# Order of the expert loop in a mixture-of-experts block: gathers three experts ahead, transposes before the down products

## The chip, the cores and the metric

The kernel runs on one core of a Trainium2 chip (trn2). The metric is the device time of one execution in microseconds (us). Three runs of the kernel before gave a median of 1673.04 us (1669.24 to 1675.33).

## The reference, cut to what matters

The reference is one decoder block: a mixer half (not touched by the change) and a routed mixture of experts over 512 tokens of width 1024. Every token is routed to 8 of 64 experts, and every expert is a SwiGLU layer of hidden width 256:

```python
def expert_block(args):
    toks, ws, e = args
    xb = u_pad[toks]                                             # gather the tokens of this expert
    hid = jax.nn.silu(xb @ we_gate[e]) * (xb @ we_up[e])         # (128, 256)
    return (hid @ we_down[e]) * ws[:, None]                      # (128, 1024), scaled by the routing weight
routed = jax.ops.segment_sum(y_slots, slot_tok, num_segments=N + 1)[:N]
```

All arithmetic is float32. The number of tokens of an expert is known only on the chip.

## The kernel before, in words

The expert loop (`experts`, lines 1075 to 1295) is unrolled over the 64 experts, in an order written out by hand. Each engine runs its own instructions in that order and waits on semaphores for the others. What an expert does depends on its token count `n`, which each engine reads into a register; `tc.If` then gives branches on each engine that has work in them:

- **light** (`n <= 64`): the float32 weights are used as they were loaded. gate and up products in float32 (`gate_up_light`, L976), one copy of the sums to `hid` by ScalarE (L1185), two transposes of `hid` by TensorE (`hidden_in`, L1008), silu and product after them (`hidden_turned`, L1225 and L1226), down products (`down_light`, L985).
- **heavy** (`n > 64`): each of the three weight units (`gu[e][0]`, `gu[e][1]`, `dn[e]`, 1 MB each) is first split into a high and a low float32r part: a copy by ScalarE (L45) and a subtraction by VectorE (L46), 128x2048 each. The products are then three float32r matmuls each (`mm3`, L61 to L63). silu and product stand ahead of the transposes (`gate_act`, L998 and L999), and the transposed hidden values are split again (`hidden_out`, L1014 and L1015).
- **two blocks** (`n > 128`): a heavy expert with a second block of tokens: it is gathered, transposed, multiplied and scattered besides the first.

The tokens of expert `e` are gathered by an indirect DMA on the POOL queue (`fetch`, and `fetch_over` for the second block) into `xg`, transposed by TensorE (`turn_in`, L899, 8 transposes) into the two PSUM buffers of `xt`, and evicted (`turned`: L1202 for a light expert, the split pair L909 and L910 for a heavy one). `downs(e - 1)` is one expert behind: the down products of the first block of the expert before. The result is added into DRAM by an indirect DMA on the POOL queue (`scatter`, L1044). The loads of expert `e + 2` are issued by SyncE at the end of the iteration (L946, L947, L953) into 8 raw buffers of 1 MB, used in turn, three for each expert.

In iteration `e` the order before is: gathers of `e + 2`; split of the next expert's first unit; products of `e`; second products; transposes of `e + 1`; their eviction and the split of the next expert's second unit, in one branch; transposes of the second block of `e + 1`; down products of `e - 1`; transposes of `hid` of `e`; second down products with their own transposes; scatters; loads. A fifth product (`index_part`, L858, bf16, small) makes the slot numbers of expert `e + 4`.

Where a value is written in only one of two branches, the other branch counts the semaphore up instead, at its line of `If` (L1160 is that of `by_count`, L1169 of `if_two`, L1176 of `if_heavy`).

Of the kernel before, what the change touches and what calls it, by code (L numbers as in the profile page):

```python
# [11 lines left out]
F32 = mybir.dt.float32  # L12
# [9 lines left out]
P = 128  # L22
T = 512
NT = 4
# [34 lines left out]
def mm3(k, out, sh, sl, mh, ml, first, last):  # L59
    nc = k.nc  # L60
    nc.tensor.matmul(out, sh, mh, start=first, stop=False)  # L61
    nc.tensor.matmul(out, sh, ml, start=False, stop=False)  # L62
    nc.tensor.matmul(out, sl, mh, start=False, stop=last)  # L63
# [788 lines left out]
    return oh  # L852


def slot_product(k, ps, oh, vv, b):

    for t in range(NT):
        k.nc.tensor.matmul(ps[:, b, 0:5], oh[:, t, b, :], vv[:, t, :], start=t == 0, stop=t == NT - 1)  # L858


# [23 lines left out]
def gather(k, idx, b, xg, n=P):  # L884
    k.nc.gpsimd.indirect_dma_start(out=xg[:n], out_offset=None, in_=k.u2d, bounds_check=T - 1, oob_is_err=False,  # L885
                                   in_offset=bass.IndirectOffsetOnAxis(ap=idx[0][:n, b:b + 1], axis=0))
    return xg


def turn_tiles(k):  # L890
    return [k.xt.tile([P, 512], F32, name="xt", tag="xt").rearrange("p (q t) -> p q t", q=4) for _ in range(2)]


def turn_in(k, src, halves):

    xv = src.rearrange("p (q k) -> p k q", k=NK)
    for hf, pv in enumerate(halves):
        for q in range(4):
            k.nc.tensor.transpose(pv[:, q, :], xv[:, hf * 4 + q, :], k.ident)  # L899


def turn_out(k, halves, x, full=None):

    nc = k.nc
    for hf, pv in enumerate(halves):
        ks = slice(hf * 4, hf * 4 + 4)
        if full is not None:
            nc.scalar.copy(full[:, ks, :], pv)
        nc.scalar.copy(x[0][:, ks, :], pv)  # L909
        nc.vector.tensor_sub(x[1][:, ks, :], pv, x[0][:, ks, :].bitcast(F32))  # L910
    return x


def turn(k, src, x, full=None):
    halves = turn_tiles(k)
    turn_in(k, src, halves)
    return turn_out(k, halves, x, full)
# [39 lines left out]
def gate_up_mm(k, x, units, ps=None, halves=(0, 1)):  # L957
    xh, xl = x
    if ps is None:
        ps = k.gu.tile([P, 512], F32, name="gu", tag="gu")  # L960
    for hf in halves:
        h, l = (w.rearrange("p (s k f) -> p k s f", k=4, s=2) for w in (units[hf].h, units[hf].l))
        pv = ps.rearrange("p (s f) -> p s f", s=2)
        for q in range(4):
            kk = hf * 4 + q
            mm3(k, pv, xh[:, kk, :], xl[:, kk, :], h[:, q], l[:, q], kk == 0, kk == NK - 1)
    return ps
# [35 lines left out]
def hidden_in(k, hid, ps=None):  # L1003

    hv = hid.rearrange("p (q j) -> p j q", j=2)
    ps = k.ht.tile([P, 2, P], F32, name="ht", tag="ht") if ps is None else ps
    for j in range(2):
        k.nc.tensor.transpose(ps[:, j, :], hv[:, j, :], k.ident)  # L1008
    return ps


def hidden_out(k, ps, hx):
    nc = k.nc
    nc.scalar.copy(hx[0], ps)  # L1014
    nc.vector.tensor_sub(hx[1], ps, hx[0].bitcast(F32))  # L1015
# [59 lines left out]
def experts(k, shared):  # L1075
    nc, tc, a = k.nc, k.tc, k.a
    ET = mybir.EngineType
    idx, xg, gu, dn, oh, counts = {}, {}, {}, {}, {}, {}
# [42 lines left out]
    def first(e, move):  # L1121
        sized(count(e), (16, 32, 48, 64, 80, 96, 112, P), move)
# [9 lines left out]
    def fetch(e):  # L1132
        if e < E:
            xg[e] = k.xg[e % 2]
            first(e, lambda n: gather(k, idx[e], 0, xg[e], n))

    def fetch_over(e):
        if e < E:
            second(e, lambda n: gather(k, idx[e], 1, k.xg[3 + e % 2], n))
# [13 lines left out]
    every, both = (ET.PE, ET.Activation, ET.DVE), (ET.Activation, ET.DVE)  # L1153

    def by_count(e, engines, light, heavy):

        if e == 0:
            heavy()
        elif e < E:
            with tc.If(count(e, engines) <= LIGHT) as small:  # L1160
                light()
            with small.Else():
                heavy()

    def if_two(e, two, one=lambda: None):

        if e == E:
            return one()
        with tc.If(count(e, every) > P) as more:  # L1169
            two()  # L1170
        with more.Else():
            one()

    def if_heavy(e, engines, body):
        if e < E:
            with tc.If(count(e, engines) > LIGHT):  # L1176
                body()

    def products(e):

        g, hid = k.gu.tile([P, 512], F32, name="gu", tag="gu"), hidden(k)

        def light():
            gate_up_light(k, k.xf, gu[e], g)
            nc.scalar.copy(hid, g[:, :256])  # L1185

        def heavy():
            gate_up_mm(k, k.xT[e % 2], gu[e], g)
            if e > 0:
                dn[e].split(k, k.dnw[e % 2])  # L1190
            gate_act(k, g, hid)

        by_count(e, every, light, heavy)
        return hid

    def turned(e, halves):

        if e == E:
            return
        def light():  # L1200
            for hf, pv in enumerate(halves):
                nc.scalar.copy(k.xf[:, hf * 4:hf * 4 + 4, :], pv[:, :, :LIGHT])  # L1202

        def heavy():
            turn_out(k, halves, k.xT[e % 2])
            gu[e][1].split(k, k.gu1w)

        by_count(e, both, light, heavy)

    def downs(e):  # L1210
        if e < 0:
# [6 lines left out]

        by_count(e, every, lambda: down_light(k, k.hT, dn[e], y, w), heavy)

    def hidden_turned(e, hid):
        ps = hidden_in(k, hid)

        def light():
            nc.scalar.activation(k.hT, ps[:, :, :LIGHT], AF.Silu)  # L1225
            nc.vector.tensor_mul(k.hT, k.hT, ps[:, :, LIGHT:])  # L1226

        by_count(e, both, light, lambda: hidden_out(k, ps, k.hx[e % 2]))

    with tc.manual_schedule():  # L1230
        fetch_over(0)
        fetch_over(1)
        if_two(0, lambda: turn(k, k.xg[3], k.xT[1]))
        for e in range(E):
            fetch(e + 2)
            fetch_over(e + 2)
            onehot(e + 4)
            for i in (e, e + 1):
                if i < E:
                    for engines in (every, both):  # L1240
                        count(i, engines)
            if_heavy(e + 1, both, lambda: gu[e + 1][0].split(k, k.gu0w[(e + 1) % 2]))
            hid = products(e)
            hid1, halves = hidden(k), turn_tiles(k)
            slots = slot_tile(k, 2) if e + 4 < E else None

            def turns():
                if e + 1 < E:
                    turn_in(k, xg[e + 1], halves)

            def second_products():
                gate_act(k, gate_up_mm(k, k.xT[(e + 1) % 2], gu[e]), hid1)
                turns()

            def index_part(b):
                if e + 4 < E:
                    slot_product(k, slots, oh[e + 4], k.V[:, :, e + 4, :], b)

            def next_second():
                index_part(0)  # L1260
                turn(k, k.xg[3 + (e + 1) % 2], k.xT[e % 2])

            def second_down():
                ps = turn_tiles(k)[0].rearrange("p q t -> p (q t)")[:, :2 * P].rearrange("p (j t) -> p j t", j=2)
                hidden_in(k, hid1, ps)
                index_part(1)
                hidden_out(k, ps, k.hx[2])
                for n in range(2):
                    down(k, k.hx[2], dn[e], n, k.xg[2], idx[e][1][:, 1:2])

            if_two(e, second_products, turns)
            turned(e + 1, halves)
            if_two(e + 1, next_second, lambda: index_part(0))
            downs(e - 1)
            hidden_turned(e, hid)
            if_two(e, second_down, lambda: index_part(1))
            if e > 0:
                first(e - 1, lambda n: scatter(k, idx[e - 1], 0, k.yl[(e - 1) % 2], (e - 1) % 2, n))
            second(e, lambda n: scatter(k, idx[e], 1, k.xg[2], e % 2, n))
            load(e + 2)  # L1280
            if e + 4 < E:
                idx[e + 4] = slot_numbers(k, slots, 2)
        e = E - 1
        downs(e)
        first(e, lambda n: scatter(k, idx[e], 0, k.yl[e % 2], 1, n))
        part = k.part = [token_pair(k, k.Y[0], t) for t in (0, 2)]
        for t in range(NT):
            eng = (nc.vector, nc.gpsimd)[t % 2]
            y, h = (u[t // 2][:, t % 2, :] for u in (part, k.hs2))
            eng.tensor_mul(y, y, k.rows[:, 0, :])  # L1290
            eng.tensor_add(h, h, y)  # L1291
# [183 lines left out]
```

## Time and profile before

| | |
|---|---|
| median of three runs | 1673.04 us (1669.24 to 1675.33) |
| the profiled execution, its time | 1673.0 us |
| its span, first to last instruction | 1671.3 us |
| mean granted TensorE clock | 0.947 of full |
| DMA over the span | 340.32 MB, 204 GB/s |
| DMA from 800 to 1630 us (the expert loop) | 230.93 MB, 278 GB/s |

The mixer, the norm, the router and the shared expert end at about 808 us; the expert loop runs from there to about 1628 us, and the output follows. Engines: PE is TensorE's matmul, PEld its weight load, DVE VectorE, ACT ScalarE, POOL GpSimd, SP SyncE. A name with q (DVEq) is the engine's sequencer: a branch or a semaphore.

### The profile page before, as it was taken

Reading aid. Unit: us, or ns where it says so; the run is one execution under the profiler, and the core shown is the slowest. Engines: PE = TensorE matmul, PEld = TensorE weight load, DVE = VectorE, ACT = ScalarE, POOL = GpSimd, SP = SyncE. Lnnn points to the kernel's source line nnn. Section 1 sums busy time; section 2 is a strip of 40 time slices with the busy share of each in tenths; the row PEclk is TensorE's granted clock in tenths of the full one; section 3 lists DMA queues with packets and bytes.
Section 4 is the critical chain, followed back from the end, with each engine's and each line's share of the span. In section 5 each row is a group of like instructions: output and inputs, shape, how many; then the busy total and the mean of one; then the engine's idle time right before and its main releaser. Section 6 shows DMA issues by size and latency. Waiting matters only on the chain. (4 is left out here: it accounts for less than half of the span.)

```text
span 1671.3 us, 25992 instructions
## 1 busy us (share of the span) xinstructions
PE 1475.4 (88%) x8084; PEld 1156.2 (69%) x8084; DVE 1011.8 (61%) x1744; ACT 745.2 (45%) x1027; POOL 370.3 (22%) x312
## 2 busy tenths in 40 slices
PE   5999999999999999999898888898798888887970
PEld 5888788788888778888675666566576665665640
DVE  6889778778877974558743354545436453355326
ACT  3465546454434223325544455444536454355332
POOL 5201101002010111220122322322324222221226
PEclk7999999999999999999999999899899989898995
DMA  9442433243333236236738778958889999898974
GB/s 288 122 126 76 138 102 121 76 126 101 107 105 117 82 114 233 87 115 227 294 113 285 252 235 289 329 189 258 282 251 313 324 329 318 287 325 273 297 288 151
DMA packets 152127, 340.32 MB, mean 204 GB/s; under 512 B 15816, under 2 KB 94832, under 8 KB 142272
## 3 DMA queue, kind: packets, MB, share of 16 engines
q1 hardware_dynamic: 135888, 294.94, 51.8%
q0 software_dynamic: 15408, 40.23, 9.4%
q8 instruction: 118, 1.93, 0.5%
q10 hardware_dynamic: 576, 2.10, 0.3%
q14 instruction: 137, 1.12, 0.2%
HBM read 314.00 MB, written 31.01 MB: 206 GB/s over the span
## 5 line engine op out<-in xcount | busy, mean ns | idle before, releaser
L46 DVE TENSOR_TENSOR wl<-raw,wh 128x2048 fp32r<-128x2048 f32 x114 | 273.5, 2404 | 100.0 <-ACT wh L45 88.4
L45 ACT CAST wh<-raw 128x2048 fp32r<-128x2048 f32 x114 | 216.6, 1906 | 140.3 <-PE mm L62 65.7
L1044 POOL DMA_INDIRECT Y<-yl,idx x64 | 108.2, 1691 | 481.8 <-ACT yl L988 271.9
L61 PE MATMUL mm<-uh,wh 128*128 128x512 f32 x432 | 171.7, 397 | 1.9 <-ACT zs L285 1.9
L63 PE MATMUL mm<-uh,wl 128*128 128x512 f32 x432 | 170.4, 395 | 0.0
L62 PE MATMUL mm<-ul,wh 128*128 128x512 f32 x432 | 169.8, 393 | 0.0
L899 PE MATMUL xt<-ident,xg 128*128 128x128 f32 x632 | 97.2, 300 | 58.2 <-issue 18.6
L899 PEld LDWEIGHTS xt<-ident,xg 128*128 128x128 f32 x632 | 84.9, 196 | 77.7 <-issue 48.9
L976 PE MATMUL gu<-raw,xf 128*64 128x256 f32 x1056 | 125.9, 387 | 6.1 <-DMA raw<-in_we_up_dram 3.5
L885 POOL DMA_INDIRECT xg<-u2d,idx x75 | 93.5, 1247 | 117.5 <-DVE oh L851 36.4
L46 DVE TENSOR_TENSOR pair<-raw,pair 128x2048 fp32r<-128x2048 f32 x33 | 75.0, 2290 | 58.2 <-ACT pair L45 49.7
L976 PEld LDWEIGHTS gu<-raw,xf 128*64 128x64 f32 x1056 | 77.2, 138 | 42.6 <-issue 7.2
L61 PE MATMUL gu<-wh,xh 128*128 128x512 f32 x256 | 103.1, 403 | 1.0 <-ACT xh L909 0.6
L62 PE MATMUL gu<-wl,xh 128*128 128x512 f32 x256 | 101.9, 398 | 0.7 <-DVEq L1169 0.7
L63 PE MATMUL gu<-wh,xl 128*128 128x512 f32 x256 | 101.3, 396 | 0.0
L1226 DVE TENSOR_TENSOR hT<-hT,ht 128x128 f32<-128x128 f32 x33 | 9.5, 288 | 146.8 <-ACTq L1169 142.5
L61 PEld LDWEIGHTS mm<-uh,wh 128*128 128x128 f32 x432 | 81.6, 189 | 20.4 <-ACT zs L285 2.3
L63 PEld LDWEIGHTS mm<-uh,wl 128*128 128x128 f32 x432 | 81.6, 189 | 17.7 <-issue 0.9
L62 PEld LDWEIGHTS mm<-ul,wh 128*128 128x128 f32 x432 | 81.5, 189 | 16.8 <-issue 0.4
L45 ACT CAST pair<-raw 128x2048 fp32r<-128x2048 f32 x33 | 62.1, 1903 | 61.7 <-DMA raw<-in_we_gate_dram 22.8
L985 PE MATMUL yo<-raw,hT 128*64 128x512 f32 x264 | 75.5, 695 | 3.5 <-DMA raw<-in_we_gate_dram 2.0
L327 DVE SCALAR_TENSOR_TENSOR cv<-mm,cw,cv 128x511 f32<-128x511 f32 (+2 forms) x90 | 66.6, 741 | 2.1 <-ACT cv L324 1.8
(354 smaller groups left out, 3336.8 us busy)
## 6 DMA issues: line engine op xcount, KB each, us to landing
raw<-in_we_gate_dram SPq DMA_DIRECT2D x124, 512.0 KB
raw<-in_we_up_dram SPq DMA_DIRECT2D x124, 512.0 KB
raw<-in_we_down_dram SPq DMA_DIRECT2D x62, 1024.0 KB
raw<-in_w_in_dram SPq DMA_DIRECT2D x27, 1024.0 KB
raw<-in_w_ada_dram SPq DMA_DIRECT2D x16, 1024.0 KB
big<-in_w_ada_dram SPq DMA_DIRECT2D x16, 512.0 KB
raw<-in_w_in_dram SPq DMA_DIRECT2D x16, 512.0 KB
raw<-in_w_br_ssd_dram SPq DMA_DIRECT2D x8, 1024.0 KB
```

Of the source, the lines that this page charges most:

```text
L45: nc.scalar.copy(h, raw)
L46: nc.vector.tensor_sub(l, raw, h.bitcast(F32))
L61: nc.tensor.matmul(out, sh, mh, start=first, stop=False)
L62: nc.tensor.matmul(out, sh, ml, start=False, stop=False)
L63: nc.tensor.matmul(out, sl, mh, start=False, stop=last)
L327: nc.vector.scalar_tensor_tensor(cv[:, sft:], ps[:, :T - sft], k.cw[:, j * 32 + blk:j * 32 + blk + 1], cv[:, sft:], op0=ALU.mult, op1=ALU.add)
L885: k.nc.gpsimd.indirect_dma_start(out=xg[:n], out_offset=None, in_=k.u2d, bounds_check=T - 1, oob_is_err=False, in_offset=bass.IndirectOffs ...
L899: k.nc.tensor.transpose(pv[:, q, :], xv[:, hf * 4 + q, :], k.ident)
L976: nc.tensor.matmul(ps[s * LIGHT:(s + 1) * LIGHT, :256], x[:, kk, :], w[:, s, kk % 4, :], start=kk == 0, stop=kk == NK - 1)
L985: nc.tensor.matmul(ps[n * LIGHT:(n + 1) * LIGHT, :], x[:, j, :], unit.raw[:, j * D + n * 512:j * D + n * 512 + 512], start=j == 0, stop=j ...
L1044: k.nc.gpsimd.indirect_dma_start(out=k.Y[acc], out_offset=bass.IndirectOffsetOnAxis(ap=idx[0][:n, b:b + 1], axis=0), in_=y[:n], in_offset= ...
L1226: nc.vector.tensor_mul(k.hT, k.hT, ps[:, :, LIGHT:])
```

## The change

Five things change in the loop; the arithmetic is the same.

1. `fetch` and `fetch_over` are called for `e + 3` near the end of iteration `e` (ahead of its scatters) and no longer for `e + 2` at its start; those of expert 2 are called ahead of the loop.
2. The split of the next expert's first unit moves into the branches of `products`: in a heavy expert it is first, in a light one it comes after the copy of `hid`.
3. The split of the next expert's second unit leaves the branch of `turned` and gets an `If` of its own, behind the second block's hidden transposes.
4. The transposes of `hid` come right after those of the next expert's tokens, ahead of `downs(e - 1)`. Those of a second block come next, into a buffer of `gu` and no longer of `xt`, with their eviction.
5. The transposes of the next expert's second block come after `downs(e - 1)`; the second block's down products are last. The index products are dealt out differently.

```diff
         def light():
             gate_up_light(k, k.xf, gu[e], g)
             nc.scalar.copy(hid, g[:, :256])
+            next_split()
 
         def heavy():
+            next_split()
             gate_up_mm(k, k.xT[e % 2], gu[e], g)
...
-        def heavy():
-            turn_out(k, halves, k.xT[e % 2])
-            gu[e][1].split(k, k.gu1w)
-
-        by_count(e, both, light, heavy)
+        by_count(e, both, light, lambda: turn_out(k, halves, k.xT[e % 2]))
...
+        fetch(2)
+        fetch_over(2)
         for e in range(E):
-            fetch(e + 2)
-            fetch_over(e + 2)
             onehot(e + 4)
...
-            if_heavy(e + 1, both, lambda: gu[e + 1][0].split(k, k.gu0w[(e + 1) % 2]))
             hid = products(e)
...
+            def second_turned():
+                ps = k.gu.tile([P, 512], F32, name="gu", tag="gu")[:, :2 * P].rearrange("p (j t) -> p j t", j=2)
+                hidden_in(k, hid1, ps)
+                index_part(0, (0, 1))
+                hidden_out(k, ps, k.hx[2])
+
             def next_second():
-                index_part(0)
                 turn(k, k.xg[3 + (e + 1) % 2], k.xT[e % 2])
+                index_part(0, (2, 3))
 
             def second_down():
-                ps = turn_tiles(k)[0].rearrange("p q t -> p (q t)")[:, :2 * P].rearrange("p (j t) -> p j t", j=2)
-                hidden_in(k, hid1, ps)
                 index_part(1)
-                hidden_out(k, ps, k.hx[2])
                 for n in range(2):
                     down(k, k.hx[2], dn[e], n, k.xg[2], idx[e][1][:, 1:2])
 
             if_two(e, second_products, turns)
             turned(e + 1, halves)
-            if_two(e + 1, next_second, lambda: index_part(0))
+            ps = hidden_in(k, hid)
+            if_two(e, second_turned, lambda: index_part(0, (0, 1)))
+            if_heavy(e + 1, both, lambda: gu[e + 1][1].split(k, k.gu1w))
             downs(e - 1)
-            hidden_turned(e, hid)
+            hidden_turned(e, ps)
+            if_two(e + 1, next_second, lambda: index_part(0, (2, 3)))
             if_two(e, second_down, lambda: index_part(1))
+            fetch(e + 3)
+            fetch_over(e + 3)
             if e > 0:
```

`next_split()` is `if_heavy(e + 1, both, ...)` with the split of `gu[e + 1][0]`, and `slot_product` takes the token tiles that it is to work on.

## Rows read from the trace of the kernel before

**Rows 1.** Two stretches of the loop; last columns granted clock, DMA share, GB/s.

```profile
800.00:1250.00 450.00, 391.02 (x2199) 291.01 (x2198) 208.96 (x406) 210.55 (x291) 117.41 (x81) 0.94 0.77 255
1250.00:1350.00 100.00, 86.54 (x545) 62.91 (x543) 48.08 (x98) 49.99 (x70) 30.65 (x19) 0.97 0.97 320
```

**Rows 2.** TensorE's waits, 800 to 1630: total us, times, longest.

```profile
PE xt L899 <- issue: 18.6, 6, 5.4
PE xt L899 <- ACT wh L45: 16.1, 6, 6.0
PE ht L1008 <- DVEq L1160: 15.3, 5, 6.2
PE xt L899 <- DMA xg<-u2d,idx: 14.7, 12, 2.4
PE yo L61 <- ACT hh L1014: 10.0, 11, 1.4
PE ht L1008 <- DVEq L1169: 7.7, 4, 3.4
PE xt L899 <- DVE xl L910: 5.7, 1, 5.7
PE xt L1008 <- DVEq L1169: 5.3, 2, 2.7
```

**Rows 3.** Light experts' copy of `hid`: count, shortest/median/longest ns.

```profile
L1185 ACT COPY hid<-gu x33: 366/372/374, 882.5 to 1608.4; 128x256 f32<-128x256 f32 x33
```

**Rows 4.** Load issues' waits on SyncE, 800 to 1630.

```profile
SPq L946 <- PE yo L61: 243.5, 27, 26.7
SPq L946 <- PE yo L985: 144.8, 23, 14.0
```

**Rows 5.** Timeline, two blocks to two blocks (e = 2).

```profile
848.46 0.68 PE L899 MATMUL xt<-ident,xg 128*128 128x128 f32 x4 [1.08 <-ACT xh L909]
...
849.87 0.71 PE L899 MATMUL xt<-ident,xg 128*128 128x128 f32 x4 [0.72 <-ACT wh L45]
```

**Rows 6.** Timeline, light to heavy (e = 50), weights late.

```profile
1467.81 0.37 ACT L1185 COPY hid<-gu 128x256 f32<-128x256 f32 x1
1467.94 2.29 DVE L46 TENSOR_TENSOR pair<-raw,pair 128x2048 fp32r<-128x2048 f32 x1 [11.75 <-ACT pair L45]
...
1470.43 0.67 PE L1008 MATMUL ht<-ident,hid 128*128 128x128 f32 x2 [6.15 <-DVEq L1160]
```

**Rows 7.** Timeline, light to two blocks (e = 10).

```profile
965.33 2.29 DVE L46 TENSOR_TENSOR pair<-raw,pair 128x2048 fp32r<-128x2048 f32 x1 [0.45 <-ACT pair L45]
...
966.27 0.37 ACT L1185 COPY hid<-gu 128x256 f32<-128x256 f32 x1 [0.98 <-PE gu L976]
...
969.35 1.71 PE L899 MATMUL xt<-ident,xg 128*128 128x128 f32 x8 [2.12 <-issue]
...
970.99 3.25 PE L985 MATMUL yo<-raw,hT 128*64 128x512 f32 x8
...
974.61 0.48 PE L61 MATMUL gu<-pair,xh 128*128 128x512 f32 x1
```

**Rows 8.** Timeline, light to heavy (e = 14), weights early.

```profile
1016.03 1.90 ACT L45 CAST pair<-raw 128x2048 fp32r<-128x2048 f32 x1 [0.34 <-ACTq L1169]
...
1018.91 0.37 ACT L1185 COPY hid<-gu 128x256 f32<-128x256 f32 x1 [0.98 <-PE gu L976]
...
1019.80 1.94 PE L985 MATMUL yo<-raw,hT 128*64 128x512 f32 x8
...
1024.14 0.50 PE L63 MATMUL gu<-pair,xl 128*128 128x512 f32 x1 [1.31 <-issue]
```

**Rows 9.** Timeline, heavy to heavy (e = 33).

```profile
1288.50 0.41 DVE L999 TENSOR_TENSOR hid<-hid,gu 128x256 f32<-128x256 f32 x1
1289.06 0.47 PE L1008 MATMUL ht<-ident,hid 128*128 128x128 f32 x2 [2.33 <-DVEq L1169]
```

**Rows 10.** VectorE's waits at passed branches.

```profile
DVE fx L869 <- DVEq L1169: 7.3, 34, 0.5
```

More of the change, by code (lines that the diff above doesn't have):

```diff
@@ L852, in slot_onehot, with slot_product @@
     return oh
-def slot_product(k, ps, oh, vv, b):
-    for t in range(NT):
+def slot_product(k, ps, oh, vv, b, tiles=range(NT)):
+    for t in tiles:
         k.nc.tensor.matmul(ps[:, b, 0:5], oh[:, t, b, :], vv[:, t, :], start=t == 0, stop=t == NT - 1)
@@ L1181, in products, with next_split @@
         g, hid = k.gu.tile([P, 512], F32, name="gu", tag="gu"), hidden(k)
+        def next_split():
+            if_heavy(e + 1, both, lambda: gu[e + 1][0].split(k, k.gu0w[(e + 1) % 2]))
         def light():
@@ L1219, in downs, with hidden_turned @@
         by_count(e, every, lambda: down_light(k, k.hT, dn[e], y, w), heavy)
-    def hidden_turned(e, hid):
-        ps = hidden_in(k, hid)
+    def hidden_turned(e, ps):
         def light():
@@ L1253, in second_products, with index_part @@
                 turns()
-            def index_part(b):
+            def index_part(b, tiles=range(NT)):
                 if e + 4 < E:
-                    slot_product(k, slots, oh[e + 4], k.V[:, :, e + 4, :], b)
+                    slot_product(k, slots, oh[e + 4], k.V[:, :, e + 4, :], b, tiles)
+            def second_turned():
[3 more added lines that the diff above has]
+                hidden_out(k, ps, k.hx[2])
             def next_second():
-                index_part(0)
                 turn(k, k.xg[3 + (e + 1) % 2], k.xT[e % 2])
+                index_part(0, (2, 3))
             def second_down():
-                ps = turn_tiles(k)[0].rearrange("p q t -> p (q t)")[:, :2 * P].rearrange("p (j t) -> p j t", j=2)
-                hidden_in(k, hid1, ps)
                 index_part(1)
-                hidden_out(k, ps, k.hx[2])
                 for n in range(2):
```

## The prediction

> **What bounds the kernel now.** I read the windows first. From 800 to 1250 us TensorE is busy 391 of 450 us and the DMA engines 0.77 of the time; from 1250 to 1350 the DMA share is 0.97 [rows 1]. So neither fills the loop: TensorE is idle for about one eighth of it, and the DMA is the limit only in runs of light experts, where every expert's 3.1 MB take 9.8 us at the 320 GB/s of that stretch. [...]
>
> Then TensorE's waits [rows 2]. The rows of `xt L899` other than the gathers' make some 41 us: 18.6 + 16.1 + 5.7 and a small rest, less one that is another wait. On the timeline nearly all of it stands in front of the second block's transposes, 11 times. `yo <- hh` with 10.0 and `xt L1008` with 5.3 stand in the second block's down part. `ht L1008`, 15.3 + 7.7, is the hidden transposes waiting for VectorE, and 14.7 are gathers that landed late.
>
> Then the order of the experts, walked through on the timeline: 33 are light [rows 3], 20 heavy with one block, 11 have two. A light expert is followed by one of two blocks 6 times, by a heavy one 9 times; three heavy ones are followed by two blocks.
>
> Last, what the loads wait for: 243.5 + 144.8 us of SyncE's time ends with a down product [rows 4]. The three units of expert e + 2 are released in the main by `downs(e - 1)`.
>
> **A wait after an `If`.** One row decides how I cost the reordering. After light expert 50 ScalarE copied `hid` by 1468.18, and VectorE has nothing to do with it; yet TensorE's transposes began at 1470.43, just after VectorE's split of the next expert's unit ended at 1470.23 and it passed its branch (`DVEq L1160`) [rows 6]. So whoever reads a value behind an `If` waits until both engines have counted as far as the longer branch would have. In the new kernel the next split stands inside that branch, behind the copy. I expect the transposes of `hid` to wait for it still, and they now stand ahead of the down products.
>
> **Part A, experts of two blocks (11).** Their hidden transposes come early and their eviction runs under the first block's down products: the 10.0 and the 5.3 go [rows 2]. Where two such follow each other (twice), the second turn no longer waits for the split behind the eviction, 1.08 + 0.72 [rows 5], 3.6 in all. [...] What hides the new order's work: some 2 to 3 us of down products. **-20.**
>
> **Part B, light or heavy to two blocks (9).** The remaining 37 us of waiting at the second turn don't vanish. Take e = 10. Before, the split ran under the products and VectorE ended it at 967.62; the turn then had to wait until 969.35 for the eviction, and the next products began at 974.61 [rows 7]. Now the split starts after the copy: 966.64, a branch 0.35, ScalarE 1.90 [rows 8], 0.1, VectorE 2.29, which makes 971.3. [...] That is 0.7 to 2.5 later; I take 1.5, for the three with early weights. In the six where the split was late anyway, it doesn't start later, and the gap between its end and the second turn (967.62 to 969.35, 1.7) is filled with hidden transposes and down products: 1 to 4 earlier, I take 2. Together 3 x 1.5 - 6 x 2. **-7.5.**
>
> **Part C, light to heavy (9).** Here is the loss. At e = 14 the copy ended at 1019.28; split 0.35 + 1.90 + 0.1 + 2.29 to 1023.9, hidden transposes 0.5, down products 1.94, index 0.24: products from 1026.7, their third matmul 0.7 later at 1027.4. Before it was at 1024.14, a wait of 1.31 included [rows 8]. So 3.3 to 4.5 with the slow clock, 3.5 for each of four with early weights. In the five with late weights the wait was there [rows 6] and only the down products (1.94 to 3) come on top, less what the next products lose today to the clock: 1.5 each. Of the nine, three (two early, one late, 8.5 us) lead into an expert whose own product is late by 6 us or so for want of weights, which takes the loss up. 14 + 7.5 - 8.5. **+13.**
>
> **Part D, heavy experts.** `hid` of e = 33 was done at 1288.91, and the transposes waited only the last 2.33 for it, since the down products came first [rows 9]. With the transposes first that cover is gone. On the timeline about twelve such products come more than a turn (1.05) late. Were each to cost a whole set of down products, it would be 30; but VectorE's sequence is the bound of such runs and stays as it is, so that a run pays once: five runs at about 1. Bounds 0 and 30; nearer to the low one, since the waits of a run don't add up in the trace. **+5.**
>
> **Part E, the gathers.** Issued three ahead, each is on its queue behind the next expert's turn and no longer behind a scatter that waits for the down products. That takes 14.7 off [rows 2], but eight of the twelve stand where part B or C waits anyhow. **-3.5.** Queued behind the gather of a second block are now the scatters, which wait for TensorE's turn; the yl buffers they free are needed two experts later, so nothing.
>
> **Part F, branches.** There is one more `If` for each expert on TensorE and two on ScalarE and VectorE. A passed one holds VectorE 7.3 / 34 = 0.21 [rows 10]. They lie on the path only where part B and C count 0.35 for one; the rest and a tail whose last eviction is queued later: **+2.** [...]
>
> **The sum.** -20 - 7.5 + 13 + 5 - 3.5 + 2 = -11. The profiled execution took 1673.0 (span 1671.3 and 1.7 around it), as much as the median. **1662 us.**
>
> **Rivals.**
>
> *The wait ends with the copy.* If TensorE waits for the copy alone, part C falls to about 0 and part B grows to what the eviction allows (some 1.6 behind the split, in place of 4 to 6): -26. Sum -20 - 26 + 5 - 3.5 + 2 = -42: 1631. For it: the copy is put ahead of the split. Against it: [rows 6], where the copy was done for 2.2 us. Chance 0.1.
>
> *The loads come late (slower).* Each new wait at the hidden transposes holds up `downs(e - 1)`, and with it 3 MB of loads [rows 4]. In seven cases (three of B, four of C) that is 3.7 us, 26 in all. If it comes back as late weights in the next experts, -11 + 26 = +15: 1688. It decides from about 20 us that come back. For it: SyncE waits for down products nearly half of the loop. Against it: the DMA is free 0.23 of the time up to 1250 [rows 1], and an expert of two blocks, which takes twice as long, lets it catch up. Chance 0.2.
>
> *The DMA is the limit anyway.* From 1250 on its share is up to 0.97 [rows 1]; if all that comes after is swallowed, there remain about two thirds of part A and half of B, less what C costs up to there: -5, 1668. Against it: loads that are released earlier also start earlier. Chance 0.22.
>
> *Code loading.* Some TensorE waits have no releaser in the trace, and every further branch could add one; at 1 us for each fourth of 64 experts, 16: 1678. [...] The rows don't bear it out: TensorE's listed waits have other causes [rows 2], with five branches for each expert already. Chance 0.05.
>
> **How the numbers follow.** My own sum has 0.43. 0.5% is 8.4 us, about what a measurement of this kernel can tell from no change. Forecast: five in six of its cases lie beyond -8.4; the first rival is faster, the second three in four times slower, the third and fourth mostly within. Faster 0.36 + 0.1 + 0.04 = 0.50, slower 0.21, same 0.29. Range: C between 0 and 9 x 4.5 = 40, D between 0 and 30, B between -26 and +5 give both ends; 1640 to 1684 leaves out about a tenth at either side. If my sum's mechanism holds, 1653 to 1672.
>
> **What the profile would show.** Right: `yo <- hh` and the waits at the second turn nearly gone; a new, larger wait at `ht L1008` released by VectorE, about 3.5 us behind every light expert that a heavy one follows; gathers off the list. Wrong if `ht L1008` shows no more than now (first rival), if ScalarE's waits for raw weights grow by over 20 us (second), or if waits without a releaser grow (fourth).

## Result and the profile after: 1719.75 us, 2.8% slower

The median of four runs is 1719.75 us (1715.43 to 1723.56); the kernel before took 1673.78 beside it (1669.24 to 1675.33). The ratio is 1.0279, 95% interval 1.0243 to 1.0314. The forecast was 1662, range 1640 to 1684. The profiled execution has a span of 1715.2 us against 1671.3, 43.9 longer.

Of those 43.9, 41.9 lie in the expert loop: from the first product of expert 0 to that of expert 63 it is 844.3 us against 802.4. The page's first part says that no work was added to TensorE (8084 matmuls in both), and that the same work took it 20 us longer. Here is the line of the kernel before, then that of the changed one:

```profile
PE 1475.4 (88%) x8084; PEld 1156.2 (69%) x8084; DVE 1011.8 (61%) x1744; ACT 745.2 (45%) x1027; POOL 370.3 (22%) x312
```

```profile
PE 1495.8 (87%) x8084; PEld 1159.5 (68%) x8084; DVE 1013.0 (59%) x1744; ACT 745.9 (43%) x1027; POOL 352.5 (21%) x312
```

The two stretches that answer to [rows 1], same columns:

```profile
800.00:1250.00 450.00, 388.70 (x2176) 287.39 (x2176) 208.07 (x405) 210.29 (x290) 105.33 (x81) 0.93 0.77 252
1250.00:1350.00 100.00, 85.86 (x483) 62.69 (x481) 48.83 (x92) 47.65 (x64) 24.91 (x17) 0.93 0.85 274
```

In the second stretch the DMA share has fallen from 0.97 to 0.85: the DMA no longer sets the pace even there. TensorE's waits, 800 to 1675 (total us, times, longest), answer to [rows 2]:

```profile
PE ht L1008 <- DVEq L1169: 100.4, 29, 8.5
PE gu L976 <- DMA raw<-in_we_up_dram: 7.9, 6, 2.4
PE yo L61 <- ACT yl L988: 7.0, 6, 1.5
...
PE yo L61 <- ACT yl L1040: 2.5, 4, 0.6
...
PE xt L899 <- issue: 1.2, 1, 1.2
```

All waits of the second turn (the transposes of the next expert's second block) and of the gathers have gone, and one has come: the hidden transposes wait 100.4 us for VectorE, 29 times, against 15.3 + 7.7 before. The second block's down products wait as long as before, 7.0 + 2.5 in place of 10.0, now for the evictions of the first block's.

On each timeline I took the time from an expert's first gate and up matmul to the next expert's, and added these up by kind of pair (L light, H heavy, 2 two blocks). The columns to the right are experiments below.

| pair (number) | before | after | both back | second turn ahead | hidden behind | own arm |
|---|---|---|---|---|---|---|
| L to H (9) | 101.8 | 141.9 | 102.7 | 98.8 | 110.7 | 94.6 |
| L to 2 (6) | 90.3 | 95.0 | 75.7 | 91.3 | 81.8 | 76.6 |
| H to H (8) | 89.6 | 102.6 | 87.2 | 86.8 | 86.2 | 107.0 |
| H to L (8) | 83.5 | 89.5 | 79.5 | 84.4 | 82.0 | 91.8 |
| H to 2 (3) | 56.8 | 44.8 | 43.6 | 55.9 | 41.6 | 53.6 |
| 2 to 2, 2 to H (4) | 90.3 | 78.1 | 82.9 | 82.1 | 83.2 | 80.9 |
| 2 to L (7) | 135.9 | 136.2 | 141.2 | 139.4 | 137.9 | 138.5 |
| L to L (18) | 154.1 | 156.2 | 156.9 | 159.7 | 156.3 | 162.7 |

Before to after, the pairs with a two-block expert became 19.2 us shorter together; a light expert ahead of a heavy one costs 40.1 more, heavy ones ahead of heavy or light ones 19.0 more.

**Light to heavy.** The timeline at e = 14, which answers to [rows 8] (start, us, engine, line, operation, in brackets the idle time before it and what ended that):

```profile
1014.19 0.37 ACT L1188 COPY hid<-gu 128x256 f32<-128x256 f32 x1 [3.07 <-PE gu L976]
1014.46 1.90 ACT L45 CAST pair<-raw 128x2048 fp32r<-128x2048 f32 x1
...
1016.45 2.29 DVE L46 TENSOR_TENSOR pair<-raw,pair 128x2048 fp32r<-128x2048 f32 x1 [3.32 <-issue]
...
1018.89 0.67 PE L1008 MATMUL ht<-ident,hid 128*128 128x128 f32 x2 [3.82 <-DVEq L1169]
...
1019.64 3.68 PE L985 MATMUL yo<-raw,hT 128*64 128x512 f32 x8
...
1024.44 0.63 PE L63 MATMUL gu<-pair,xl 128*128 128x512 f32 x1
```

The copy is done by 1014.56, yet TensorE starts the transposes at 1018.89, right behind VectorE's subtraction. The eight down products that follow take 3.68 us; before, with nothing waiting ahead of them, they took 1.94 [rows 8]. The window of these products shows why (granted clock third from the end), and the window of the next products that the clock came back:

```profile
1019.60:1023.30 3.70, 3.66 (x9) 0.91 (x10) 3.06 (x3) 0.57 (x1) 0.00 (x0) 0.50 1.02 312
1026.00:1029.50 3.50, 3.50 (x17) 2.86 (x16) 1.38 (x7) 1.91 (x1) 0.34 (x1) 1.00 0.96 355
```

So the wait of 3.8 us was paid again by half in the products behind it, which ran at a granted clock of 0.50.

**Heavy to heavy.** The timeline from e = 33 to 34, which answers to [rows 9]:

```profile
1300.50 0.41 DVE L999 TENSOR_TENSOR hid<-hid,gu 128x256 f32<-128x256 f32 x1
1301.06 0.47 PE L1008 MATMUL ht<-ident,hid 128*128 128x128 f32 x2 [2.78 <-DVEq L1169]
...
1301.95 0.79 PE L61 MATMUL yo<-pair,hh 128*128 128x512 f32 x1 [0.32 <-issue]
...
1304.92 0.69 ACT L1040 ACTIVATE yl<-yo,wt 128x512 f32<-128x512 f32 x1 [3.05 <-PE yo L63]
...
1306.38 0.69 ACT L1040 ACTIVATE yl<-yo,wt 128x512 f32<-128x512 f32 x1 [0.78 <-PE ixp L858]
...
1308.07 3.71 ACT L45 CAST pair<-raw 128x2048 fp32r<-128x2048 f32 x2 [0.73 <-ACTq L1169]
...
1310.01 4.49 DVE L46 TENSOR_TENSOR pair<-raw,pair 128x2048 fp32r<-128x2048 f32 x2 [0.63 <-ACT pair L45]
...
1314.42 0.41 DVE L999 TENSOR_TENSOR hid<-hid,gu 128x256 f32<-128x256 f32 x1
...
1314.98 0.62 PE L1008 MATMUL ht<-ident,hid 128*128 128x128 f32 x2 [1.95 <-DVEq L1169]
```

Read it as a ring: the transposes wait for `hid`, the down products of the expert before stand behind the transposes, their evictions on ScalarE stand behind the products, ScalarE's next two splits stand behind the evictions, VectorE's behind ScalarE's, and the next `hid` behind these. One turn takes 13.9 us, from 1301.06 to 1314.98, and while TensorE runs the down products ScalarE stands idle, 3.05 us ahead of their first eviction, and splits nothing. In the kernel before, the down products needed no `hid` of the same turn, and the ring was open: the two splits behind the evictions waited for their weights, and the turn from 1289.06 [rows 9] took 11.2.

```profile
1293.32 3.70 ACT L45 CAST pair<-raw 128x2048 fp32r<-128x2048 f32 x2 [2.10 <-DMA raw<-in_we_up_dram]
...
1300.23 0.48 PE L1008 MATMUL ht<-ident,hid 128*128 128x128 f32 x2 [0.81 <-DVEq L1169]
```

### The profile page after: what moved, and what is told of

Read it like the earlier page. It is cut to its first block, busy times and chain, and to the rows that moved or that the text cites. A ratio compares the mean times of both kernels' runs of the same rounds, so it can differ in the third digit from the quotient of the medians.

```text
span 1715.2 us, 26579 instructions
## 1 busy us (share of the span) xinstructions
PE 1495.8 (87%) x8084; PEld 1159.5 (68%) x8084; DVE 1013.0 (59%) x1744; ACT 745.9 (43%) x1027; POOL 352.5 (21%) x312
## 5 line engine op out<-in xcount | busy, mean ns | idle before, releaser
L885 POOL DMA_INDIRECT xg<-u2d,idx x75 | 90.0, 1201 | 351.8 <-PE ht L1008 117.6
L1044 POOL DMA_INDIRECT Y<-yl,idx x64 | 93.8, 1466 | 328.6 <-ACT yl L988 184.0
L976 PE MATMUL gu<-raw,xf 128*64 128x256 f32 x1056 | 130.3, 389 | 15.3 <-DMA raw<-in_we_up_dram 7.9
L1008 PE MATMUL ht<-ident,hid 128*128 128x128 f32 x136 | 32.8, 327 | 101.9 <-DVEq L1169 100.4
L63 PE MATMUL gu<-wh,xl 128*128 128x512 f32 x256 | 100.4, 392 | 0.0
L899 PEld LDWEIGHTS xt<-ident,xg 128*128 128x128 f32 x632 | 80.5, 193 | 26.9 <-issue 21.5
L1008 PEld LDWEIGHTS ht<-ident,hid 128*128 128x128 f32 x136 | 21.6, 205 | 108.6 <-issue 89.5
L985 PE MATMUL yo<-raw,hT 128*64 128x512 f32 x264 | 88.2, 802 | 6.0 <-DMA raw<-in_we_gate_dram 2.4
L899 PE MATMUL xt<-ident,xg 128*128 128x128 f32 x632 | 88.7, 284 | 1.5 <-issue 1.2
```

The source lines that it names most:

```text
L976: nc.tensor.matmul(ps[s * LIGHT:(s + 1) * LIGHT, :256], x[:, kk, :], w[:, s, kk % 4, :], start=kk == 0, stop=kk == NK - 1)
L985: nc.tensor.matmul(ps[n * LIGHT:(n + 1) * LIGHT, :], x[:, j, :], unit.raw[:, j * D + n * 512:j * D + n * 512 + 512], start=j == 0, stop=j ...
L1044: k.nc.gpsimd.indirect_dma_start(out=k.Y[acc], out_offset=bass.IndirectOffsetOnAxis(ap=idx[0][:n, b:b + 1], axis=0), in_=y[:n], in_offset= ...
```

## Experiments

I held that the hidden transposes ahead of the down products are the loss (H), and against it that the split behind the light copy is (S). The first four kernels undo one part each, or two.

```diff
# split ahead: next_split() leaves both arms of products, and stands ahead of it again
+            if_heavy(e + 1, both, lambda: gu[e + 1][0].split(k, k.gu0w[(e + 1) % 2]))
             hid = products(e)
# hidden behind
-            ps = hidden_in(k, hid)
...
             downs(e - 1)
-            hidden_turned(e, ps)
+            hidden_turned(e, hidden_in(k, hid))
# gathers two ahead
+            fetch(e + 2)
+            fetch_over(e + 2)
             onehot(e + 4)
...
-            fetch(e + 3)
-            fetch_over(e + 3)
```

**Split ahead.** 

> The changed kernel with one part undone: the split of the next expert's first unit stands ahead of the products again, under an If of its own. The hidden transposes still stand ahead of the down products. Theory S (the loss is the split behind the light copy: 15 waits at ht L1008 behind light experts, about 71 of the 100.4 us): those waits fall by most of it, 1650 to 1675. Theory H (the loss is that the hidden transposes have lost their cover, wherever the split stands): only the pairs with early weights gain, some 7 times 3, the waits at ht L1008 stay above 65 us, 1695 to 1710.

1694.45 us, ratio 1.0131 (1.0111 to 1.0150): half a microsecond below H's range, and 19 above S's. The waits at `ht L1008` stay at 57.8 + 30.0.

**Hidden behind.** 

> The changed kernel with another part undone: the first block's hidden transposes stand behind the down products of the expert before again; the split stays behind the light copy. Theory H: both kinds of wait get their cover back, in heavy runs too, ht L1008 falls from 100.4 to some 30 to 45 us, 1655 to 1685. Theory S: 15 pairs keep 1.5 to 2 us each of the late split, the heavy runs were never the matter, 1695 to 1710.

1646.62 us, 0.9831 (0.9815 to 0.9847): 73 us less than the changed kernel, and faster than before. S is out. H has the direction, but the time is 8 below its range, and the waits that are left are more than the 30 to 45 that it named:

```profile
PE ht L1008 <- DVEq L1169: 54.1, 19, 9.5
```

In the profiled execution, the slowest of five (1653.33), the span is 63.6 shorter: these waits are 46 less, and TensorE's busy time is 22 less (1473.5 in place of 1495.8, for the same matmuls at a mean granted clock of 0.953 in place of 0.939).

**Both back.** 

> Both undone; what stays of the change is the second block's early hidden transposes, the second turn behind the down products, the split of the second unit under its own If, and the gathers three ahead. H and S together (these two are the whole loss): faster than before by part A and E of the prediction's sum, 1645 to 1665. If another part loses too (the second turn behind the down products, further branches, gathers ahead of scatters): 1670 or more.

1640.26 us, 0.9799 (0.9781 to 0.9818): the fastest of all, 33 below the kernel before, and below what H and S named as its floor. The split's place is worth 25 us with the hidden transposes ahead (1720 to 1694), 6 with them behind (1647 to 1640): there the down products cover most of the wait.

**Gathers two ahead.** 

> The changed kernel with the gathers issued two ahead, at the head of the turn, as in the kernel before. If gathers three ahead gain what the prediction's part E says, or up to the 14.7 us of waits for xg in the kernel before: 1723 to 1733, with xt waits for xg back in the list. If they cost (scatters and releases held up behind gathers that wait for TensorE): 1700 to 1712. If neither: 1716 to 1722.

1718.05 us, 1.0248 (1.0215 to 1.0281). No difference that can be told, although the late gathers are back:

```profile
PE xt L899 <- DMA xg<-u2d,idx: 13.9, 8, 3.3
```

The next question was which experts lose. Two kernels put the transposes ahead of the down products for one kind alone; a third has the same branches, and the transposes always behind.

```diff
-            ps = hidden_in(k, hid)
+            ps = k.ht.tile([P, 2, P], F32, name="ht", tag="ht")
+            by_count(e, every, lambda: hidden_in(k, hid, ps), lambda: None)   # light ahead
...
             downs(e - 1)
+            by_count(e, every, lambda: None, lambda: hidden_in(k, hid, ps))
```

**Light ahead.** 

> The changed kernel, with the first block's hidden transposes ahead of the down products only where the expert is light; a heavy or two-block expert transposes behind them. Behind them everywhere was 1647, ahead everywhere 1720: 73 us to share out. Theory H-light (the 15 waits behind light experts, 71 of the 100 us at ht L1008, are nearly the whole loss): 1690 to 1710. Theory H-loop (heavy runs lose as much, since each heavy expert's hidden copy then waits for the evictions of the down products, which wait for the transposes): 1670 to 1690.

1721.61 us, 1.0307 (1.0263 to 1.0351), above both expectations: as slow as with all of them ahead.

**Heavy ahead.** 

> The counterpart: ahead only where the expert is heavy or of two blocks, light ones transpose behind the down products. H-light, and the prediction's part D (+5): 1650 to 1662. H-loop: 1670 to 1690. If both parts are independent, this and its counterpart lie 73 us above 1647 together.

1689.43 us, 1.0105 (1.0069 to 1.0141), at the upper end of H-loop.

**Neither ahead, same branches.** 

> The control for the two runs that split light from heavy: the same two further branches for each expert, but the hidden transposes behind the down products whatever the expert is (an empty If ahead of them, an If with the transposes in both arms behind). Theory B (the two branches cost by themselves, since TensorE's row ixp <- PEq L1160 gave 21.6 us over 31 times and 35.1 over 53 in those runs): 1668 to 1685 against 1647 without them, so that light ahead costs some 40 to 50 and heavy ahead some 5 to 20. Rival (branches are free, and light and heavy together simply cost more than both at once): 1644 to 1655.

1649.56 us, 0.9842 (0.9805 to 0.9880): as without the branches (1646.62). Against this control light ahead costs 72 and heavy ahead 40, 112 in place of 73. It isn't a good control. In the other two, one arm of each `If` holds no transposes. There TensorE's sequencer counts the semaphore up in their stead, and first it waits for TensorE's own count. These are its rows with heavy ahead; with light ahead there are 63 such counts too, in the control none, although there as well an arm with transposes is jumped over in every turn but the first:

```profile
L1160 PEldq COMPARE_BRANCH  x351: 67/176/982, 815.6 to 1636.5; - x176
L1160 PEldq EVENT_SEMAPHORE  x63: 51/51/51, 831.6 to 1635.9; - x63
```

The branches that follow such a count are passed only then, and TensorE stands idle meanwhile. Its waits in the run with heavy ahead:

```profile
PE ht L1008 <- DVEq L1169: 39.2, 21, 6.1
PE ixp L858 <- PEq L1160: 35.1, 53, 1.0
```

That is 0.66 us for each, 35.1 in all. With light ahead it is 21.6 over 31 times, 22 of them in the turn of a light expert. The 39 us that the two runs cost beyond 73 may well lie there; how much of them does, no run shows. The split between the kinds is read better inside one trace: with light ahead, heavy to heavy falls to 84.3 us, and light to heavy is 147.6; with heavy ahead, light to heavy is 101.9, as before, and heavy to heavy 106.7. Both kinds lose. By the table (after against hidden behind) the pairs that a light expert leads, to a heavy one or one of two blocks, make 44 us, those that a heavy one leads 27, and those of two blocks give 7 back.

**The ring.** One run put the hidden copy, its subtraction or the SiLU ahead of the evictions; another cut a split out of the ring.

```diff
# hidden copy ahead (two hT buffers)
+            hidden_turned(e, ps)
             downs(e - 1)
-            hidden_turned(e, ps)
# hid ahead of the down split
             gate_up_mm(k, k.xT[e % 2], gu[e], g)
+            gate_act(k, g, hid)
             if e > 0:
                 dn[e].split(k, k.dnw[e % 2])
-            gate_act(k, g, hid)
```

> The changed kernel with the first block's hidden copy, subtraction or SiLU put ahead of the evictions of the down products on ScalarE and VectorE (light experts alternate between two hidden buffers, the second block's hid lies in its output tile). H-loop: the loop through the evictions is cut, runs of heavy experts go from 13 to 14.7 us per expert to about 11, 1690 to 1705; the waits behind light experts stay. Rival (the loss in heavy runs is the bare wait for VectorE's product): 1712 to 1722.

1730.83 us, 1.0332 (1.0291 to 1.0372), outside both expectations. To make room for the second hT buffer, its shared expert, ahead of the loop, was left with one buffer for `hid`, and the loop began at 820.3 in place of 810.3. With a second place for it:

> The run with the hidden copy ahead of the evictions (1731), mended in the same way (its loop began at 820.3). If the hidden copy's place in the queue is no part of the loss: 1716 to 1723, as the changed kernel. If it cuts the chain of the heavy runs: below 1712.

1719.35 us, 1.0276 (1.0244 to 1.0308): as the changed kernel, and heavy to heavy 102.5 as in it. So the hidden copy is no link of the ring; that form of my theory fell. The links that are left are the evictions and the splits queued behind them, and the next run takes one split (2.29 us on VectorE) out:

> The changed kernel with one edit: in a heavy expert the SiLU and the product for hid stand ahead of the split of its down weights, so VectorE makes hid 2.3 us earlier (one 128x2048 subtraction). Theory H-loop' (in heavy runs the chain is hid, transposes, down products, their evictions, then on ScalarE and VectorE the next split and the down split, then the next hid; cutting one split out of it takes about 2 us off each turn of it): heavy runs fall from 13 to 14.7 us per expert to about 11, 1695 to 1708. Rival (VectorE's sum of work sets the pace, so that the split only moves behind hid and delays the next products as much): 1714 to 1725.

1702.99 us, 1.0161 (1.0131 to 1.0192): 17 back, as expected of the ring. Heavy to heavy falls from 102.6 to 88.1, heavy to two blocks from 44.8 to 40.1; heavy to light rises from 89.5 to 92.8. So `hid` is held up by the split ahead of it. A mere wait behind that split would give as much back, without any ring; a run with the evictions themselves behind the splits, which would tell the two apart, was not tried.

**The join.** Does TensorE wait for the data, or for the end of the branch that holds the split? A light expert gets a `hid` tile of its own, and TensorE's transposes an arm of their own. The order of the work stays; to make room, the second block's `hid` moves into that block's output tile.

```diff
-            nc.scalar.copy(hid, g[:, :256])
+            nc.scalar.copy(k.lid, g[:, :256])
...
-            ps = hidden_in(k, hid)
+            ps = k.ht.tile([P, 2, P], F32, name="ht", tag="ht")
+            by_count(e, every, lambda: hidden_in(k, k.lid, ps), lambda: hidden_in(k, hid, ps))
```

> The changed kernel, but a light expert's evicted product has a tile of its own, and TensorE's transposes stand in an If of their own with an arm for each, so that the light arm waits for ScalarE's copy alone and not for the end of the branch that also holds the next split. The order of the work is that of the changed kernel. Theory J (TensorE waits for the join of the branch, not for the data): the 71 us behind light experts fall below 20, the next products then wait for the split itself, so that the cover of the down products comes back: 1665 to 1690. Rival (the wait is for the data, or it only moves on to the next products in full): 1712 to 1722.

1692.45 us, 1.0114 (1.0073 to 1.0155), outside both expectations by 2 us, with the same late start of the loop (821.2). With a second place for the shared expert's `hid`:

> The run with the light expert's own tile and arm (1692), with the shared expert's hid alternating between two places again; with one place the expert loop began at 821.2 in place of 810.3. Nothing in the loop differs. Theory J: the waits at ht L1008 behind light experts stay gone and the time is 1692 less 10 to 12: 1678 to 1685. If the late start was made up later: 1688 to 1695.

1681.66 us, 1.0063 (1.0041 to 1.0084): 38 less than the changed kernel with the work in the same order. The moved tiles are not the reason: the run at 1719.35 above moves the same ones. Its waits:

```profile
PE ht L1008 <- DVEq L1169: 35.2, 16, 5.6
PE xt L899 <- issue: 17.1, 5, 6.6
PE gu L61 <- DVEq L1169: 13.0, 7, 3.9
```

All 35.2 at `ht L1008` are heavy experts' now; light to heavy is 94.6, less than before the change. Of the 65 us that have gone from there, 30 come back in the lower two rows, which are the second turn and the next products waiting for the same split: this part was data all along. And heavy to heavy goes up further, to 107.0.

In the two kernels with the transposes behind, the arm was added as well, with the one buffer ahead of the loop:

> The kernel at 1647 (hidden transposes behind the down products, split behind the light copy) with the light expert's own tile and arm as in the run before. Theory J: the waits at ht L1008 that are left there (54.1 us, 19 times) fall to the heavy ones' share, some 10 to 15, but mostly reappear as waits of the next products, which need the same split: 1635 to 1650. If the further branch costs more than that gives: 1650 to 1662.

1665.56 us, 0.9933 (0.9906 to 0.9960), above both expectations. The waits at `ht L1008` fall from 54.1 to 4.7, and come back in full at the next products and the second turn:

```profile
PE gu L61 <- DVEq L1169: 33.0, 11, 5.9
PE xt L899 <- issue: 23.8, 4, 9.6
```

> The kernel at 1640 (both back) with the light expert's own tile and arm. Here the split stands ahead of the copy on ScalarE, so that the arm frees TensorE of VectorE's split alone: 42.6 us of waits at ht L1008 are left to win, most of them late weights that the next products wait for in any case. Theory J: 1628 to 1642. If the branch costs more: 1642 to 1655.

1660.96 us, 0.9902 (0.9866 to 0.9938), above both expectations. By the medians the two are 19 and 21 us slower than without the arm. Some 9 and 12 of that are the loops' late start (820.3 against 811.4, 820.4 against 808.8); the arm itself costs the rest, some 10 and 9. Behind the down products it has nothing to win.

**Where the 33 come from.** Last, the kernel at 1640 with one part more undone.

```diff
             if_two(e, second_turned, lambda: index_part(0, (0, 1)))
+            if_two(e + 1, next_second, lambda: index_part(0, (2, 3)))
...
             downs(e - 1)
             hidden_turned(e, hidden_in(k, hid))
-            if_two(e + 1, next_second, lambda: index_part(0, (2, 3)))
```

> The kernel at 1640 (both parts back) with the second block's turn ahead of the down products again, as in the kernel before. If the gain of 33 us comes from the second block's hidden transposes alone (the prediction's part A): 1638 to 1648. If the second turn behind the down products carries its part (B, the waits at xt behind ScalarE's split and eviction, 18.6 + 16.1 + 5.7 in the kernel before): 1652 to 1668, with those waits back in the list.

1671.33 us, 1.0007 (0.9992 to 1.0023): slower than either expectation, and all 33 gone. Its waits at `xt`, then those of the kernel at 1640, where they had turned into smaller ones at `ht`:

```profile
PE xt L899 <- issue: 37.7, 8, 11.5
PE ht L1008 <- DVEq L1160: 20.1, 6, 5.9
PE xt L899 <- DVE xl L910: 7.2, 1, 7.2
```

```profile
PE ht L1008 <- DVEq L1160: 32.7, 9, 8.5
PE ht L1008 <- DVEq L1169: 9.9, 8, 4.0
...
PE xt L899 <- DVE xl L910: 2.1, 3, 0.9
PE xt L899 <- ACT wh L45: 2.1, 3, 1.1
```

One edit, then, carries the whole gain: the second turn behind the down products, which it had kept waiting. The second block's early transposes, the `If` of the second unit's split and the gathers bring nothing together.

> The kernel at 1640 with the gathers two ahead, as before. Where no larger wait stands over them, the 14.7 us of late gathers of the kernel before should show: 1646 to 1656. If they are covered here too: 1637 to 1644.

1640.86 us, 0.9813 (0.9794 to 0.9832). Gathers three ahead are worth nothing here either; the waits for `xg` come back with 13.8 us, and others shrink in their place (`ht L1008 <- DVEq L1160` to 26.5).

## Why the prediction was wrong

The sum was -11, measured on the profiled execution it is +43.9. By the table of pairs:

- **Part C failed, with 27 of the 55 us.** Its mechanism was right: behind a light expert TensorE waits for the join of the branch with the split in it, and the run with an arm of its own shows it. The size was not: +13 forecast, +40.1 measured. At e = 14 the transposes came 4.3 us behind the copy's end, the forecast's 4.6. But I took the down products at 1.94, as in the kernel before, where the granted clock was 1.00 in them, though they stand right behind a wait of 3.8; they took 3.68 at 0.50. From the copy's end to the third matmul it went from 4.86 [rows 8] to 9.88: 5.0 in place of the 3.5 taken (the forecast's path with the 1.94, added again, gives 3.2). And e = 14 was the mildest of the four early cases: its 4.86 holds a wait of 1.31 that the other three don't have. They went from 3.96, 4.12 and 4.17 to 11.28, 10.25 and 11.22, in two of them with a heavy expert's down products (3.0 us before) and not a light one's 1.94. The four early cases lengthened by 25 in place of 14, the five late ones by 15 in place of 7.5; what the next products of these lose to the clock, which the forecast took off, no run shows. The 8.5 that I took off, because the next expert waits for weights anyhow, did not come; by ScalarE's rows at the end of this section the waits for weights had themselves become shorter. The bound of 40 that the range gave to this part was reached.
- **Part D failed, with 14.** "VectorE's sequence is the bound of such runs and stays as it is, so that a run pays once" was the wrong step: +5, where +19.0 was measured. The moved transposes close a ring, and every turn of it pays. The bounds 0 and 30 held; I chose the wrong end. That `hid` waits for a split is shown by the run with that split put behind it; that the chain closes over the evictions is read from the timeline and was not tried.
- **Part A was 8 too high.** -12.2 measured, in the four pairs where a two-block expert is followed by a heavy one or another of two blocks. In the seven ahead of a light one, nothing (135.9 to 136.2). "The 10.0 go" was wrong: `yo` waits for the first block's evictions as long as it had for `hh`, 9.5 against 10.0. I had named the work that hides the eviction, and not that this work has evictions of its own in the same two buffers. The -20 has 1.1 more than 10.0, 5.3 and 3.6 make, for a slower clock behind the waits; no run shows the 1.1. The trace of the kernel before shows a granted clock of 0.54 from 850.60 to 853.00, behind the 1.08 + 0.72 at e = 2 [rows 5].
- **Part B came out at its number, -7.5, by luck.** Measured are -12.0 for heavy to two blocks and +4.7 for light to two blocks, where the forecast had +1.5 for each of three and -2 for each of six. Its path for e = 10 took the down products at 1.94 [rows 8] to 3.25 [rows 7], with a granted clock of 1.00 and of 0.59 in the kernel before, and came to 975.3 to 977.1 for the next products, against 974.61 (added again, it is 0.1 shorter); the 1.5 taken from that no run shows. With the transposes behind the down products the same move is worth -31 (1671 to 1640).
- **Parts E and F:** -1.5 forecast, some +4 in what is left (light to light, two blocks to light, the start and the tail). Gathers are nothing, in two runs.

**The rivals.** That the wait ends with the copy did not come about; made to come about, with the arm, it gave 1681.7 and not 1631, since 30 of the 71 us of wait behind light experts are for the split itself, and the heavy experts' ring is still closed. Late loads were wrong too: SyncE does wait longer for the down products,

```profile
SPq L946 <- PE yo L61: 262.9, 28, 21.8
SPq L946 <- PE yo L985: 180.0, 23, 12.5
```

443 us against 388 [rows 4], but ScalarE waits less for raw weights. These are the kernel before's three largest such rows, then the changed kernel's:

```profile
ACT wh L45 <- DMA raw<-in_we_up_dram: 47.4, 17, 9.7
...
ACT pair L45 <- DMA raw<-in_we_gate_dram: 22.8, 8, 9.0
ACT pair L45 <- DMA raw<-in_we_up_dram: 20.7, 4, 11.7
```

```profile
ACT wh L45 <- DMA raw<-in_we_up_dram: 15.8, 11, 4.6
...
ACT wh L45 <- DMA raw<-in_we_gate_dram: 11.3, 11, 2.2
...
ACT pair L45 <- DMA raw<-in_we_gate_dram: 7.8, 7, 2.7
```

The slower loop left the DMA more time: from 1250 to 1350 us its share was 0.85 in place of 0.97. For the same reason the DMA was no limit. Waits of TensorE without a releaser did not grow (27 us before, 8 after). That [rows 2] spoke against code loading was misread, though: their largest row, 18.6, is one without a releaser. It went with the second turn's place, and came back with it (37.7 in the run at 1671).

## What to carry to other kernels

When work is moved ahead of a block that covered its wait, cost the wait at full length, and the block behind it at the clock that such a wait left here (0.50 behind one of 3.8 us), not the one that it has today. Ask of every such move whether it closes a ring over a whole turn of the loop: if what is moved waits for the end of one engine's queue, and that queue waits for what now stands behind it, each turn pays (by the timelines here 13.9 us in place of 11.2). And an edit of several moves is taken apart by undoing them one at a time: here one move was worth -31 us, a second +54 or +73 and a third +6 or +25, each by where the other stood, and the rest nothing that can be told.

## What the runs showed of the hardware

An arm of an `If` that holds no work for TensorE held it up. In the two runs that split light from heavy, its sequencer stood 63 times in such an arm and waited for TensorE's own count. Behind that TensorE stood idle ahead of the index products 0.66 us on average with heavy ahead (35.1 us over 53 times) and 0.70 with light ahead (21.6 over 31). The control's branches (27010 instructions in place of 26533), whose list of waits has no such row, cost nothing that can be told (1649.56 against 1646.62 us).

The compare-and-branches of TensorE's sequencer at L1160 took 176 ns in the median with heavy ahead (351 of them, 67 to 982).
